# Four small edits to the order of work in a one-core encoder layer: VectorE for the first low parts, longer counted filter taps, a sixth early gate, pinned splits

## The chip, the cores and the metric

The kernel runs on one core of a Trainium2 chip. The metric is the device time of one execution in microseconds; smaller is better. The program has one launch and no arithmetic on the host.

## The reference: what is computed

One layer of a streaming Conformer with two mixers, on 2048 prompt rows and 64 sample rows (2112 in all), in float32, with D = 1024, eight heads of 64, 512 filter channels and an FFN of 2816. Cut to its core:

```python
sh1, sc1, gt1, sh2, sc2, gt2 = split(silu(c) @ w_ada + b_ada, 6)
h = rms_norm(x, norm1_g) * (1 + sc1) + sh1
glu_a, glu_b, q, k, v, g_conv, g_attn = split(h @ w_in)          # 512 512 512 512 512 1024 1024
u = glu_a * sigmoid(glu_b)
y = depthwise_conv(concat([hist, u]), w_dw) + b_dw               # 31 taps, causal, each channel alone
conv_out = silu(layer_norm(y, conv_ln_g, conv_ln_b)) @ w_conv_out
q, k = rms_norm(q per head), rms_norm(k per head)
s = q @ k.T / 8 + rel_bias[clip(distance, -128, 128)]            # own chunk of 64 and the 8 before it
attn_out = softmax(masked s) @ v @ w_attn_out
x = x + gt1 * ((sigmoid(g_conv) * conv_out + sigmoid(g_attn) * attn_out) @ w_o)
h2 = rms_norm(x, norm2_g) * (1 + sc2) + sh2
gate, up = split(h2 @ w_ffn_in)
y_out = x + gt2 * ((silu(gate) * up) @ w_ffn_out)
```

The sample rows have modulation, filter history and keys of their own. The last 30 filter inputs and the last keys and values are outputs as well.

## The kernel before

**Precision.** Each float32 product is made of three TensorE matmuls on operands that are split into a high part (ScalarE's copy to the short type `fp32r`) and a low part (operand minus high part, a subtraction). `mm3` issues hi x hi, hi x lo, lo x hi, in this order, so the low part of the left operand is needed by the third matmul.

**Phase 1** walks four row blocks (`PBLOCKS`, 576 or 512 rows) through the stages of `ORDER`: q, filter channels 0, k, 1, v, 2, 3, and then the two branch gates, g. The first block begins with the modulation columns `A` and `B` (small VectorE steps on `cols`), which make the transposed input `h` with its halves `hh` and `hl` and the first q product. `glu` makes 128 filter channels, `convolve` filters them with 31 VectorE instructions that all update one tile `y` (480 of them are the `scalar_tensor_tensor` form), and `conv_norm` makes the LayerNorm once the four channel groups are there and stores the result to `c_d`. Attention runs beside: `sc` are the scores, `pr` the exponentials, `sm` the row statistics, `ptp` the transposed probabilities, `o_p` the output of a head.

**Phase 2** walks three row blocks (`CBLOCKS`, 704, 640, 768 rows). Each makes the two branch projections and their merge in two chunks (`merge`), multiplies by `w_o`, and then runs one generator `residual` per 128 rows, a "turn": residual, norm, transposes into `pw`, and the split into FFN operands. The FFN's gate and up projections multiply 2 x 2 blocks (two halves of the rows, two halves of D) with seven products in place of eight, after Winograd, so the operands are `b11`, `b21`, `b22` and the sums `t1` to `t4` of the rows, and the weights `a11`, `a12`, `a22` and the sums `s1` to `s4`. GpSimd makes the sums of weights in `Weights.operand` (tile `ws`) in the first row block, and they are stored to `sum_d`, from where the other two blocks load them.

**The early gates.** The products with `a11` and `a12` need only `b11` and `b21`, which are ready before the `t` operands. For the first `EARLY` = 5 of the 22 slabs of 128 FFN columns they are done ahead: `first(f)` (with `a11`, key `fi`, 12 matmuls into a bank of tag `y`, of which there are four, then a copy to the tile `early`) and `second(f)` (with `a12`, 12 matmuls, then SiLU). Three firsts and two seconds come before the rest of the turns is drained, `first(3), first(4), second(2), second(3), second(4)` after it, with a call of `W.fill()` behind each. The main loop `up(f)` then starts at f = 0 with `s3` times `t3`; for f of 5 and more it does `a11` and `a12` itself.

**The order of the work.** Instructions are emitted by one Python program, which keeps a planned clock: every operation adds an estimate to `Stream.load` of its engine (`Meter`, `Stream.add`: a VectorE step on n elements counts 75 + 1.04 n ns), and no engine's clock stands behind TensorE's. Side work lives in generators on `Lane`s, which are pumped whenever TensorE's planned clock has moved by 500 ns; the lane of filter taps goes on while VectorE's planned clock is at most `CONV_ROOM` = 2000 ns ahead of TensorE's, up to four taps at a time. `conv.drain()` emits what is left at fixed places: at channel group 0 of the next block and, in the last block, at gate 10 (`SIDE_G`), just before the loads of the next phase (`load_mixed`, tile `cin`). `Stream.at` puts a step at a planned time. Behind the emission the tile framework orders the instructions of each engine by its own estimates, so the order of an engine is not that of the emission unless an edge demands it.

**The weights.** `Weights` loads slabs into three staging buffers (`wst`) by SyncE's queue, splits each into `whi` and `wlo` (five buffers each), stores the halves that later blocks need, and loads them from there. `split` chooses who makes the low part: VectorE for the slabs of `w_in` from the fifth on (`i >= 4`) and for every second slab of `w_o`, GpSimd for the rest. `fill` makes the next splits while a buffer is free and `available` agrees: while `hold` is set no `up` slab is split, and while turns are left (`careful`) a first `up` slab is split only if its loads and weight sums are there by the planned clock. `self.made` keeps the planned time of each sum, and `fill` is called then and when a slab has landed. `then`, at the planned end of a split, stores the halves and calls `presum`, which makes the next weight sums.

Of the kernel before, what the change touches and what calls it, by code (L numbers as in the profile page):

```python
# [8 lines left out]
F32 = mybir.dt.float32  # L9
# [7 lines left out]
P = 128  # L17
# [40 lines left out]
SCORE_ROOM = {"dve": 2500}  # L58
TURN_NS = 600.0
KEPT = ("qkv", "in", "fi", "fo")  # L60
EARLY = 5


def token_tiles(lo, hi):
# [185 lines left out]
class Weights:  # L250
# [2 lines left out]

    def __init__(self, engines, pool, dram, stream, keys, source, staging, held, kept):
        self.stream = stream
        self.sync, self.act, self.dve, self.gps = engines
        self.pool, self.dram, self.keys, self.source = pool, dram, keys, source
        self.staging, self.held = staging, held  # L260
        self.sum_pool, self.sum_d, self.sums, self.hold, self.landed = None, None, {}, 0, {}
        self.made, self.careful = {}, lambda: False
        self.room, self.leaving = {"wst": staging, "wup": 0, "wfo": 0}, {"wst": 0, "wup": 0, "wfo": 0}
        times, raws = {}, {}
        self.items, self.users, self.need, self.first, self.stored = [], [], {}, set(), {}
# [64 lines left out]
    def load(self, kind, sure=True):  # L330
        tag = self.free_tag(kind, sure)
        i = self.due[kind].pop(0)
        srcs, a, b = self.source(self.items[i])
        pool, bufs = (self.pool, self.staging) if tag == "wst" else (self.sum_pool, self.extra[tag])
        st = pool.tile([P, a, b], F32, tag=tag, name=tag, bufs=bufs)
        for j, src in enumerate(srcs):
            self.sync.dma_start(st[:, j * a // len(srcs) : (j + 1) * a // len(srcs)], src)
        self.loaded[i] = st, tag
        self.room[tag] -= 1
        self.landed[i] = self.stream.load["pe"] + DMA_LAG  # L340
        if self.items[i][0] == "fi":
            self.stream.at(self.landed[i], self.presum, True)
            self.stream.at(self.landed[i], self.fill, True)
        self.fill()

    def load_on(self, kind):
# [19 lines left out]
    def operand(self, f, op):  # L366
# [6 lines left out]
        while len(made) < int(op[1]):  # L373
            j = len(made)
            t = self.sum_pool.tile([P, 4, P], F32, tag="ws", name="ws", bufs=4)
            x, y, e = (
                lambda: (u[:, :4], u[:, 4:], ALU.add), lambda: (made[0], g[:, :4], ALU.subtract),
                lambda: (g[:, :4], u[:, :4], ALU.subtract), lambda: (g[:, 4:], made[1], ALU.subtract),
            )[j]()
            self.gps.tensor_tensor(t, x, y, e)  # L380
            made.append(t)
            self.made[f, j] = self.stream.when("pool")
            self.stream.at(self.made[f, j], self.fill, True)
            for c in self.parts_of(f, f"s{j + 1}"):
                self.drop(self.raws[c], "pool")
            self.stream.at(
                self.stream.when("pool"), lambda j=j, t=t: self.sync.dma_start(self.sum_d[f][j], t), True
            )
# [10 lines left out]
    def split(self):  # L399
# [10 lines left out]
        if not its:  # L410
            for t, d in zip((hi, lo), self.stored[key][0]):
                self.sync.dma_start(t.bitcast(F32), d)
            return
        e, name = (self.dve, "dve") if i >= 4 and key[0] in ("in", "qkv") or key[0] == "wo" and key[1] % 2 else (self.gps, "pool")
        if i in self.first:
            parts = [(slice(4 * j, 4 * j + 4), self.operand(f, op)) for j, (f, op) in enumerate(key[1:])]
            self.stream.after("act", "pool")
# [1 line left out]
            n = 4 if key[0] == "fi" else shape[1]  # L419
            parts = [(slice(j, j + n), self.loaded[its[0]][0][:, j : j + n]) for j in range(0, shape[1], n)]  # L420
        for c, src in parts:
            self.act.activation(hi[:, c], src, AF.Copy)
            self.stream.after(name, "act")
            e.tensor_tensor(lo[:, c], src, hi[:, c].bitcast(F32), ALU.subtract)
        if i in self.first:
# [17 lines left out]
    def available(self):  # L443
        i = len(self.ready)
        if i >= len(self.keys):
            return False
        if i in self.need:
            now = self.stream.load["pe"]
            if not self.there(i) or self.hold and self.keys[i][0] == "up":
                return False  # L450
            if i not in self.first or not self.careful():
                return True
            return all(self.landed[j] <= now for j in self.need[i]) and all(
                self.made.get((f, int(op[1]) - 1), 1e18) <= now for f, op in self.keys[i][1:] if op[0] == "s"
            )
        return self.keys[i] in self.stored

    def fill(self):
# [75 lines left out]
def streaming_layer(ctx: ExitStack, tc: tile.TileContext, I, O):  # L534
    nc = tc.nc
# [572 lines left out]
    def convolve(u, y, ct, b):  # L1108
# [13 lines left out]
        dve.tensor_scalar(y[:, ct, :n], u[:, :n], wd[:, ct, 0:1], bdw[:, ct : ct + 1], ALU.mult, ALU.add)  # L1122
        for k in range(1, TAPS):
            dve.scalar_tensor_tensor(y[:, ct, :n], u[:, k : k + n], wd[:, ct, k : k + 1], y[:, ct, :n], ALU.mult, ALU.add)
            yield

    def conv_norm(y, c0, n, t0):
# [304 lines left out]
    xs = first_rows()  # L1432
    M = Slabs(nc.sync, wa, stream, list(mod_order()), source, 4)
    M.fill()
    W = Weights((nc.sync, act, dve, gps), wpool, dram, stream, list(weight_order()), source, 3, 5, lambda key: key[0] in KEPT)
    first_block(xs)
    norm_lane.add(cached_kv())
    mods = mod_steps()
# [63 lines left out]
    work = Lane({}, 600.0)  # L1502
    turns = Lane({}, TURN_NS, wide=2)
    stream.lanes = [turns, work]

    W.careful = lambda: bool(turns.gens)

    def drain():
        turns.drain()
# [130 lines left out]
    for s, (lo, hi) in enumerate(CBLOCKS):  # L1640
# [52 lines left out]
                turns.add(gens[i])  # L1693

        hid = [wk.tile([P, 2, 2, CW], F32R, tag="m0", name="hid"), None]
        early = wk.tile([P, 2 * EARLY - 2, CW // 2], F32, tag="m1", name="early")
        early = [[early[:, 2 * f + j] for j in range(2)] for f in range(EARLY - 1)]
        early.append([piece("t2", "early") for _ in range(2)])
        acc = [None] * len(tiles)

        def product(ps, w, b, first, last):
# [167 lines left out]
        if not s:  # L1869
            W.open("fo", "wfo")  # L1870
        turns.drain()
        for step, f in ((first, 3), (first, 4), (second, 2), (second, 3), (second, 4)):
            step(f)
            W.fill()
        for f in range(0, NF, 2):
# [48 lines left out]
```

## Time and profile before

| | |
|---|---|
| Time, median of 3 runs | 3055.79 us (3053.33 to 3057.89) |
| The profiled execution's own time | 3054.2 us |
| Its span | 3052.4 us |
| Its mean granted TensorE clock | 0.988 |
| TensorE busy | 2961.2 us, 16403 matmuls |
| VectorE busy | 1781.9 us, 3431 instructions |
| ScalarE busy | 1179.4 us, 2110 instructions |
| GpSimd busy | 1044.0 us, 646 instructions |
| Filter taps (480 instructions of VectorE) | 368.4 us, mean 771 ns |
| Moved by DMA | 676.27 MB, mean 222 GB/s |

The span is the profiler's, from the first to the last instruction of the core; the time of the execution has 1.8 us around it. Busy times are sums over instructions of one execution. "PEld" in the rows is the loading of weights into TensorE, which runs beside its matmuls; DVE is VectorE, ACT is ScalarE, POOL is GpSimd, SP is SyncE, whose queue issues the DMAs. The granted clock is TensorE's as a share of full speed. L101 is the line of a helper through which every operation goes, so tiles, not lines, tell the operations apart.

### The profile page before, as it was taken

Reading aid. Unit: us, or ns where it says so; the run is one execution under the profiler, and the core shown is the slowest. Engines: PE = TensorE matmul, PEld = TensorE weight load, DVE = VectorE, ACT = ScalarE, POOL = GpSimd, SP = SyncE. Lnnn points to the kernel's source line nnn. Section 1 sums busy time; section 2 is a strip of 40 time slices with the busy share of each in tenths; the row PEclk is TensorE's granted clock in tenths of the full one; section 3 lists DMA queues with packets and bytes.
Section 4 is the critical chain, followed back from the end, with each engine's and each line's share of the span. In section 5 each row is a group of like instructions: output and inputs, shape, how many; then the busy total and the mean of one; then the engine's idle time right before and its main releaser. Section 6 shows DMA issues by size and latency. Waiting matters only on the chain.

```text
span 3052.4 us, 44465 instructions
## 1 busy us (share of the span) xinstructions
PE 2961.2 (97%) x16403; PEld 2634.7 (86%) x16403; DVE 1781.9 (58%) x3431; ACT 1179.4 (39%) x2110; POOL 1044.0 (34%) x646
## 2 busy tenths in 40 slices
PE   6989898999999999998999999999999999999999
PEld 4879776888888788898999998989999999999998
DVE  4798677877977895454443436554444556343345
ACT  2324532353245257455334343443333244322321
POOL 1300120111011102348778774344445343333431
PEclk9999999999999999999999999999999999999999
DMA  9788788887987689867455469754444965333434
GB/s 309 259 290 290 244 276 268 279 266 255 310 283 247 232 277 285 267 229 238 168 188 175 149 206 332 240 175 152 152 152 142 343 209 194 125 116 129 139 113 160
DMA packets 480167, 676.27 MB, mean 222 GB/s; under 512 B 37716, under 2 KB 316104, under 8 KB 479949
## 3 DMA queue, kind: packets, MB, share of 16 engines
q1 hardware_dynamic: 467669, 656.04, 65.3%
q10 hardware_dynamic: 12280, 17.39, 1.6%
q8 instruction: 129, 2.11, 0.3%
q14 instruction: 89, 0.73, 0.1%
HBM read 501.70 MB, written 171.61 MB: 221 GB/s over the span
## 4 chain that ended last, share of the span: by engine, by line
PE 82%; DVE 10%; DMA 3%; POOL 2%; issue 1%; ACT 1%; SPq 0%; ACTq 0%; DVEq 0%; POOLq 0%
PE ps L101 52%; PE pd L101 17%; PE pw L101 6%; DVE y L101 4%; PE po L101 2%; PE sc L101 2%; PE ptp L101 2%; PE pt L101 1%; DVE pr L101 1%; POOL r L101 1%; PE pa L101 1%; POOL wlo L101 1%; DVE wlo L101 1%; ACT whi L101 0%; DMA tg<-g_d 0%
## 5 line engine op out<-in xcount | busy, mean ns | idle before, releaser
L101 POOL TENSOR_TENSOR wlo<-wst,whi 128x1024 fp32r<-128x1024 f32 (+1 forms) x217 | 461.2, 2135 | 597.0 <-ACT whi L101 482.9
L101 PE MATMUL ps<-t,whi 128*128 128x352 f32 (+2 forms) x2112 | 510.1, 325 | 9.0 <-ACT t L101 4.9
L101 PE MATMUL pd<-whi,hid 128*128 128x512 f32 (+1 forms) x1496 | 466.2, 390 | 0.0
L101 ACT ACTIVATE whi<-wst 128x1024 fp32r<-128x1024 f32 (+1 forms) x270 | 260.5, 973 | 456.7 <-PE pd L101 180.3
L101 PE MATMUL ps<-b,whi 128*128 128x352 f32 (+2 forms) x1584 | 381.4, 324 | 2.3 <-ACT early L101 1.7
L101 PEld LDWEIGHTS ps<-t,whi 128*128 128x128 f32 x2112 | 371.2, 189 | 13.7 <-ACT t L101 5.7
L101 DVE SCALAR_TENSOR_TENSOR y<-u,wd,y 128x512 f32<-128x512 f32 (+1 forms) x480 | 368.4, 771 | 6.5
L101 PE MATMUL ps<-hh,whi 128*128 128x512 f32 (+2 forms) x992 | 364.7, 368 | 0.0
L101 PE MATMUL ps<-hl,whi 128*128 128x512 f32 (+2 forms) x992 | 347.6, 350 | 0.0
L101 PE MATMUL ps<-hh,wlo 128*128 128x512 f32 (+2 forms) x992 | 346.6, 349 | 0.4 <-DVE wlo L101 0.4
L101 PE MATMUL ps<-t,wlo 128*128 128x352 f32 (+2 forms) x1056 | 342.0, 324 | 0.1
L101 PEld LDWEIGHTS pd<-whi,hid 128*128 128x128 f32 (+1 forms) x1496 | 276.1, 185 | 62.7 <-issue 0.3
L101 DVE TENSOR_TENSOR acc<-acc,pd 128x512 f32<-128x512 f32 (+1 forms) x272 | 186.9, 687 | 207.6 <-PE pd L101 206.8
L101 PE MATMUL pd<-wlo,hid 128*128 128x512 f32 (+1 forms) x748 | 291.9, 390 | 0.7 <-DMA wlo<-w_dfo_l 0.7
L101 PEld LDWEIGHTS ps<-b,whi 128*128 128x128 f32 x1584 | 276.6, 188 | 3.9 <-ACT early L101 2.7
L101 PE MATMUL ps<-b,wlo 128*128 128x352 f32 (+2 forms) x792 | 256.3, 324 | 0.0
L101 POOL TENSOR_TENSOR r<-t,mhalf 128x8 f32<-128x8 f32 (+3 forms) x68 | 86.9, 1280 | 400.4 <-DVE t L101 384.1
L101 POOL TENSOR_TENSOR wlo<-wup,whi 128x1024 fp32r<-128x1024 f32 (+1 forms) x73 | 158.8, 2176 | 171.5 <-ACT whi L101 170.4
L101 PEld LDWEIGHTS ps<-hh,wlo 128*128 128x128 f32 x992 | 188.4, 190 | 23.2 <-DVE wlo L101 0.6
L101 PEld LDWEIGHTS ps<-hh,whi 128*128 128x128 f32 x992 | 189.3, 191 | 18.5 <-issue 2.1
L101 PEld LDWEIGHTS ps<-hl,whi 128*128 128x128 f32 x992 | 189.3, 191 | 15.5 <-issue 1.7
L101 PEld LDWEIGHTS ps<-t,wlo 128*128 128x128 f32 x1056 | 200.3, 190 | 0.4 <-POOL wlo L101 0.4
(206 smaller groups left out, 5431.1 us busy)
## 6 DMA issues: line engine op xcount, KB each, us to landing
whi<-w_din_h SPq DMA_DIRECT2D x72, 512.0 KB, 6.6
wlo<-w_din_l SPq DMA_DIRECT2D x72, 512.0 KB, 6.6
wst<-sum_d SPq DMA_DIRECT2D x133, 256.0 KB, 2.9
wmod<-in_w_ada SPq DMA_DIRECT2D x48, 512.0 KB, 7.8
sum_d<-ws SPq DMA_DIRECT2D x88, 256.0 KB, 4.6
whi<-w_dfo_h SPq DMA_DIRECT2D x44, 512.0 KB, 5.2
wlo<-w_dfo_l SPq DMA_DIRECT2D x44, 512.0 KB, 6.5
wst<-in_w_ffn_in SPq DMA_DIRECT2D x83, 256.0 KB, 3.3
```

The costliest lines, as they stand in the source:

```text
L101: return f(*args, **kw)
```

## The change

Four edits, and what they take with them:

- `EARLY` is 6. The sixth early gate needs room: the tile `m1` holds the results of four early gates, the pieces `t3` and `t2` those of the fifth and sixth. The list behind the drained turns becomes first(3), first(4), second(2), second(3), first(5), second(4), second(5).
- Each tap adds 170 ns (`TAP_NS`) to VectorE's planned clock.
- The low parts of the first four slabs, too, are made by VectorE.
- ScalarE's splits of the first `up` slabs that begin with f of 0 or 1 get `tc.keep_in_program_order`: an edge that keeps the instruction behind the one that the program emitted for the same engine just before it.
- `careful`, `made` and the calls of `fill` at landing times and planned ends of sums are taken out.

```diff
@@ constants
-EARLY = 5
+EARLY = 6
+TAP_NS = 170.0
@@ Weights
-    def __init__(self, engines, pool, dram, stream, keys, source, staging, held, kept):
-        self.stream = stream
+    def __init__(self, engines, pool, dram, stream, keys, source, staging, held, kept, pin):
+        self.stream, self.pin = stream, pin
...
-        self.made, self.careful = {}, lambda: False
@@ Weights.load
             self.stream.at(self.landed[i], self.presum, True)
-            self.stream.at(self.landed[i], self.fill, True)
@@ Weights.operand
-            self.made[f, j] = self.stream.when("pool")
-            self.stream.at(self.made[f, j], self.fill, True)
@@ Weights.split
-        e, name = (self.dve, "dve") if i >= 4 and key[0] in ("in", "qkv") or key[0] == "wo" and key[1] % 2 else (self.gps, "pool")
+        e, name = (self.dve, "dve") if key[0] in ("in", "qkv") or key[0] == "wo" and key[1] % 2 else (self.gps, "pool")
...
-            self.act.activation(hi[:, c], src, AF.Copy)
+            ins = self.act.activation(hi[:, c], src, AF.Copy)
+            if i in self.first and key[1][0] < 2:
+                self.pin(ins)
@@ Weights.available
-            now = self.stream.load["pe"]
             if not self.there(i) or self.hold and self.keys[i][0] == "up":
                 return False
-            if i not in self.first or not self.careful():
-                return True
-            return all(self.landed[j] <= now for j in self.need[i]) and all(
-                self.made.get((f, int(op[1]) - 1), 1e18) <= now for f, op in self.keys[i][1:] if op[0] == "s"
-            )
+            return True
@@ convolve
             dve.scalar_tensor_tensor(y[:, ct, :n], u[:, k : k + n], wd[:, ct, k : k + 1], y[:, ct, :n], ALU.mult, ALU.add)
+            stream.load["dve"] += TAP_NS
             yield
@@ streaming_layer
-    W = Weights((nc.sync, act, dve, gps), wpool, dram, stream, list(weight_order()), source, 3, 5, lambda key: key[0] in KEPT)
+    W = Weights(
+        (nc.sync, act, dve, gps), wpool, dram, stream, list(weight_order()), source, 3, 5, lambda key: key[0] in KEPT,
+        tc.keep_in_program_order,
+    )
...
-    W.careful = lambda: bool(turns.gens)
...
-        early = wk.tile([P, 2 * EARLY - 2, CW // 2], F32, tag="m1", name="early")
-        early = [[early[:, 2 * f + j] for j in range(2)] for f in range(EARLY - 1)]
-        early.append([piece("t2", "early") for _ in range(2)])
+        early = wk.tile([P, 2 * EARLY - 4, CW // 2], F32, tag="m1", name="early")
+        early = [[early[:, 2 * f + j] for j in range(2)] for f in range(EARLY - 2)]
+        early += [[piece(tag, "early") for _ in range(2)] for tag in ("t3", "t2")]
...
-        for step, f in ((first, 3), (first, 4), (second, 2), (second, 3), (second, 4)):
+        for step, f in ((first, 3), (first, 4), (second, 2), (second, 3), (first, 5), (second, 4), (second, 5)):
             step(f)
             W.fill()
```

## The prediction

> **What bounds the kernel now.** First the page's busy shares.
>
> ```profile
> PE 2961.2 (97%) x16403; PEld 2634.7 (86%) x16403; DVE 1781.9 (58%) x3431; ACT 1179.4 (39%) x2110; POOL 1044.0 (34%) x646
> ```
>
> TensorE is busy for 2961.2 of 3052.4 us, so all its idle time together is 91.2 us, and no edit here takes a matmul away. What can be won is idle time of TensorE, and the slow clock that follows it. The view of windows tells where both lie (us, then busy time of PE, PEld, DVE, ACT and POOL, granted clock, share of DMA, GB/s):
>
> ```profile
> 0.00:50.00 50.00, 30.73 (x167) 16.83 (x171) 20.43 (x54) 15.91 (x31) 13.86 (x18) 1.00 0.90 301
> 200.00:250.00 50.00, 43.54 (x286) 40.44 (x287) 46.09 (x104) 17.67 (x42) 1.90 (x3) 0.90 0.75 255
> 450.00:550.00 100.00, 89.14 (x481) 70.63 (x481) 76.06 (x164) 22.40 (x52) 4.35 (x8) 0.91 0.84 285
> 1360.00:1425.00 65.00, 57.07 (x319) 53.58 (x318) 42.10 (x80) 39.77 (x81) 55.59 (x45) 0.95 0.77 264
> 1985.00:2010.00 25.00, 21.85 (x138) 20.65 (x137) 20.65 (x37) 14.94 (x31) 13.40 (x6) 0.93 0.57 183
> 2540.00:2600.00 60.00, 59.70 (x330) 56.67 (x329) 40.08 (x71) 33.97 (x60) 22.99 (x11) 1.00 0.55 193
> ```
>
> Four places answer to the four edits: the start, where TensorE idles 19.3 of 50 us; the filter stretches of the first phase (200 to 250, 450 to 550), idle for 17.3 us of 150 at a clock of 0.90 and 0.91; the entry to the first FFN block (1360 to 1425), idle for 7.9 us at 0.95; and the entry to the second (3.2 us at 0.93). The entry to the third has 0.3 us to give. The rows below are from the timelines of these stretches, the groups and the chain of waits.
>
> **The start: low parts of the first four slabs on VectorE.** In a timeline row stand start, duration, engine, line, operation, tiles, and in brackets the idle time before it and who ended it.
>
> ```profile
> 21.14 4.65 POOL L101 TENSOR_TENSOR wlo<-wst,whi 128x1024 fp32r<-128x1024 f32 x2 [5.76 <-ACT whi L101]
> 28.84 2.35 POOL L101 TENSOR_TENSOR wlo<-wst,whi 128x1024 fp32r<-128x1024 f32 x1 [3.05 <-ACT whi L101]
> 23.49 2.32 DVE L101 TENSOR_TENSOR A<-A,cols 128x4 f32<-128x4 f32 x1
> 43.18 0.16 DVE L101 TENSOR_TENSOR A<-A,cols 128x4 f32<-128x4 f32 x1
> 28.91 2.89 DVE L101 TENSOR_TENSOR hl<-h,hh 128x576 fp32r<-128x576 f32 x1
> 33.47 0.76 DVE L101 TENSOR_TENSOR hl<-h,hh 128x576 fp32r<-128x576 f32 x1 [0.75 <-ACT hh L101]
> 31.86 0.69 PE L101 MATMUL ps<-whi,hl 128*64 128x512 f32 x1 [1.11 <-DVE hl L101]
> 46.33 1.23 DVE L101 TENSOR_TENSOR wlo<-wst,whi 128x1024 fp32r<-128x1024 f32 x1 [0.19 <-ACT whi L101]
> ```
>
> A VectorE step on 128x4 elements takes 0.16 us at 43.18 and 2.32 us at 23.49, where it ends (25.81) within 0.02 us of the end of the two GpSimd subtractions (25.79). hl takes 0.76 at 33.47 and 2.89 at 28.91, beside the GpSimd step that begins at 28.84. VectorE stands while GpSimd works, and both steps are on the path: A makes the first h, and TensorE waits 1.11 us for hl. Without GpSimd's work the A step wins 2.16 us and TensorE's wait for hl goes, 1.11: 3.3 us. Against it, four steps of 1.23 us enter VectorE's queue; two of them become ready about when B and A do, and can push these back by some 0.4 us each. I take -2.5. The ends: all four on the path, 4.9 - 3.3 = +1.6; both VectorE delays won whole, 2.16 + 2.13 = -4.3. The four remaining slabs' DMAs and their stores stay where they are on SP's queue; the stores wait for a low part that is ready 1.1 us sooner. Everything behind follows the start, so the gain is kept.
>
> The Trainium skill has the same as a rule (SBUF — State Buffer, "Who interferes with whom"): a VectorE instruction with two SBUF inputs and a GpSimd instruction that reads SBUF exclude each other, and the later of them "fully blocks". The trace agrees, 2.32 against 0.16 us; by the rule alone this part would bring its far end, -4.3.
>
> **The filter: 170 ns more for each tap in the planner's VectorE clock.** No instruction changes; what changes is where the code puts taps between other steps, since their lane stops when VectorE's counted load is 2 us ahead of TensorE's.
>
> ```profile
> L101 DVE SCALAR_TENSOR_TENSOR y<-u,wd,y 128x512 f32<-128x512 f32 (+1 forms) x480 | 368.4, 771 | 6.5
> PE ptp L101 <- DVE pr L101: 9.9, 6, 5.9
> PE sc L101 <- DVE sm L101: 9.2, 9, 2.6
> 487.44 0.75 DVE L101 SCALAR_TENSOR_TENSOR y<-u,wd,y 128x512 f32<-128x512 f32 x1
> ...
> 488.92 0.37 DVE L101 TENSOR_SCALAR pr<-pr,sm 64x320 f32<-64x320 f32 x1
> 489.44 0.55 PE L101 MATMUL ptp<-ident,pr 64*128 64x64 f32 x3 [5.85 <-DVE pr L101]
> ```
>
> The planner counts 75 + 1.04 x 512 = 607 ns for a tap that takes 771; with 170 more it counts 777. A run of 30 taps is thus planned 30 x 0.164 = 4.9 us too short, about the longest wait (5.85 us, of softmax's small steps behind taps). From 100 to 1250 us TensorE waits 9.9 + 9.2 = 19.1 us for softmax on VectorE. The slow clock beside it, 0.10 x 50 + 0.09 x 100 = 14 us of lost clock, belongs to those waits in good part. So there are at most some 30 us to win. But VectorE's order is not the emission's: a tap needs only the tap before it, and the tool that orders each engine fills VectorE with taps wherever it thinks it free. Counting a tap 28% longer (777 / 607) thins the taps ahead of a softmax step by a fifth, not more: 0.22 x 30 = 6.6. I take -6, rounded down. The ends are -20 (two thirds) and +14 (below). What is hidden: the filter itself ends later, by the argument of the second rival.
>
> **Entry to the first FFN block: EARLY = 6, the pins, no `careful`.** `careful` held back a split of sums while turns were left. Without it nothing is emitted sooner here: until the turns are drained the sixth gate's slab takes the fifth buffer, so I cost its removal at nothing; without that cover it would move one s3 split ahead, which the pin places anyhow.
>
> ```profile
> 1380.71 1.15 ACT L101 ACTIVATE whi<-ws 128x512 fp32r<-128x512 f32 x2 [1.46 <-POOL ws L101]
> 1382.64 0.42 ACT L101 ACTIVATE pw<-pw,B,A 128x128 f32<-128x128 f32 x1
> 1387.81 0.59 PE L101 MATMUL ps<-b,whi 128*128 128x352 f32 x2 [1.58 <-ACT early L101]
> 1392.46 0.43 PE L101 MATMUL ps<-t,whi 128*128 128x352 f32 x1 [0.50 <-ACT t L101]
> 1394.81 0.66 PE L101 MATMUL ps<-t,whi 128*128 128x352 f32 x1 [1.92 <-DVE t L101]
> 1400.66 0.69 DVE L101 TENSOR_TENSOR pw<-pw,b 128x512 f32<-128x512 f32 x1
> 1405.09 0.63 ACT L101 ACTIVATE whi<-ws 128x512 fp32r<-128x512 f32 x1 [3.11 <-POOL ws L101]
> 1406.84 0.58 ACT L101 ACTIVATE t<-pw 128x512 fp32r<-128x512 f32 x1
> 1407.47 0.43 PE L101 MATMUL ps<-t,whi 128*128 128x352 f32 x1 [2.99 <-ACT t L101]
> 1408.20 17.11 PE ps L101 x95
> 1441.67 19.33 PE ps L101 x120
> L101 POOL TENSOR_TENSOR wlo<-ws,whi 128x512 fp32r<-128x512 f32 x13 | 17.0, 1325 | 0.7 <-ACT whi L101 0.7
> ```
>
> A product is 12 matmuls: 19.33 / 10 = 1.93 us. The last t operand could start when VectorE is done at 1401.35; ScalarE starts it at 1406.84, since splits of weight sums, which wait for GpSimd, stand ahead of it (1405.09, 3.11 us). That costs the 2.99 us at 1407.47. The 1.92 at 1394.81 is VectorE's own chain. The window idles 65.00 - 57.07 = 7.9 us in all and loses 0.05 x 65 = 3.2 of clock: 11 us is the ceiling.
>
> The sixth gate puts two products, 3.86 us, ahead of the first use of t; they leave the main loop (its steps a11 and a12 for f = 5), so TensorE's total stays. In block 0 GpSimd makes two more low parts first (2 x 1.325 us) and the main loop two fewer; one load and two stores of the sixth gate join SP's queue ahead of the loads that the sums need, with 0.23 of the DMA time free here. All this ends before the pinned wait below, which hides it; without that cover it would cost the 2.6 us.
>
> The pins hold the splits of f = 0 and 1 behind what ScalarE got just before them in the code. The first, s3 of f = 0, is emitted after the last t split, so it leaves its place at 1380.71 and goes behind t. This frees ScalarE: pw at 1382.64 no longer waits behind these splits and comes some 2.4 us earlier, and with it the chain to t: 1401.35 - 2.4 = 1399.0, t until 1399.5, s3's high part until 1400.1, its low part (1.325 on GpSimd) until 1401.4. TensorE has done its early products at 1392.46 - 0.50 = 1391.96 now; without the 1.58 and with 3.86 more that is 1394.2, and it waits some 7 us. The third matmul of a product takes the low part, so the first product ends near 1401.4 + 1.6 = 1403.0, and the eleven others before the first down projection at 1403.0 + 11 x 1.93 = 1424.2; at the clock lost now for each idle microsecond (3.2 / 7.9) the 7 cost 2.8 more: 1427.0. In the kernel before these twelve end at 1408.20 + 17.11 = 1425.3, with the two products still to come, so at 1429.2. That is -2. The ends are -11 (t and s3 are there when the products end) and +1 (t as late as now, until 1401.9, and the 1.58 kept: the low part at 1403.9, 8.1 us of waiting, the end at 1430.0).
>
> The Trainium skill (TensorE: Matmul & The Clock Gate, "Why this matters for your kernels") wants no TensorE gap over about 3 us, as one idle window halves the clock. Waits of 1.92 and 2.99 us came with 0.95 here, so shorter ones do it too; the rule speaks against gathering them into one wait of 7 us.
>
> **Entry to the second block.**
>
> ```profile
> 1996.43 0.41 PE L101 MATMUL ps<-t,whi 128*128 128x320 f32 x1 [1.40 <-ACT t L101]
> 2001.20 0.47 DVE L101 SCALAR_TENSOR_TENSOR early<-tg,ps 128x320 f32<-128x320 f32 x1
> ```
>
> Here sums come from DRAM and nothing is pinned. At 320 columns a product is 1.93 x 320 / 352 = 1.75 us, two are 3.5 us, against 3.2 us of idling. But four `y` banks serve six gates, so the first product with t now needs the bank of the fourth gate, whose SiLU ends at 2001.67. By then TensorE has done 12 products in place of 11. I take one product, 1.75 us, and a little clock: -2 (ends: -5, all idle time and clock, and 0). The third block has no wait to hide: 0.
>
> **Sum.** -2.5 - 6 - 2 - 2 = -12.5. The profiled execution took 3054.2 us, 1.6 less than the median of 3055.8; against the median that is 3043.
>
> **The rivals.** 0.2%, some 6 us, is about what a measurement of this kernel can tell from no change.
>
> *The planner's clock does nothing* (0.22): VectorE fills itself with taps as before, and the pinned wait eats the two products. Left are the start and the second block, -2.5 - 2 = -4.5: 3051. For it speaks that a tap already stands between softmax's small steps wherever VectorE pauses (487.44, ahead of 488.92).
>
> *The last filter runs over its drain* (0.13), slower:
>
> ```profile
> 1143.01 1.54 DVE L101 SCALAR_TENSOR_TENSOR y<-u,wd,y 128x512 f32<-128x512 f32 x2
> 1149.04 0.92 SPq L1001 DMA_DIRECT2D cin<-c_d  x2
> 1234.86 0.56 PE L101 MATMUL ps<-cin,whi 128*128 128x320 f32 x2 [1.40 <-DVE o_p L101]
> 1237.88 0.38 SPq L1181 DMA_DIRECT2D c_d<-part_l  x1
> ```
>
> The taps of the last block end at 1144.5, just before the drain whose first load is at 1149.04; its LayerNorm stores until 1237.9, while the next phase starts at 1234.86. Taps thinned by a fifth over 60 x 0.75 = 45 us end 10 to 14 us later, the rest is put in one lump before softmax, and the LayerNorm comes out behind the phase's end. It decides once the last tap passes 1149 and the wait at 1235 grows with it: +14, less 2.5 and 2 elsewhere, 3065. Against it: after 1150 VectorE is less loaded, and TensorE has gate products to do.
>
> *The waits at the FFN all close* (0.10): -11 and -5 in place of -4, 3031.
>
> **Numbers.** The forecast has 0.55 (3034 to 3049), the rivals 0.22, 0.13 and 0.10. Range 3027 to 3061. Faster 0.70 (forecast, the third rival, some of the first); same 0.18; slower 0.12.
>
> **What would show it.** Right: A<-A,cols near 25 us at about 0.16 us; TensorE idle from 0 to 100 us less by 2 to 3; waits for pr and sm from 100 to 1250 under 16 us in all; at the first FFN entry one wait of 5 to 8 us for a whi or wlo in place of three, t splits ahead of the first ws split; at the second a wait for an early bank. Wrong: waits for softmax of 20 us or more, taps after 1149 with a wait over 5 us near 1235, or splits of sums still ahead of t.

## The result and the profile after

The changed kernel takes 3073.75 us (median of 8 runs, 3064.34 to 3081.24) where the kernel before takes 3056.17 (8 runs beside it, 3046.78 to 3059.44): 1.0057 times as long, with a 95% interval of 1.0039 to 1.0075. It is slower, outside the predicted range, and the prediction had the other sign.

The profiled execution took 3073.06 us with a span of 3071.3, 18.9 more than before. First two rows of its page, the busy shares and the group with the longest waits; then the view of windows (us, busy time of PE, PEld, DVE, ACT and POOL, granted clock, share of DMA, GB/s) at the places that the prediction looked at, moved along with the later stages:

```profile
PE 2963.4 (96%) x16403; PEld 2638.0 (86%) x16403; DVE 1789.8 (58%) x3441; ACT 1176.6 (38%) x2102; POOL 1020.7 (33%) x640
L102 PE MATMUL ps<-t,whi 128*128 128x352 f32 (+2 forms) x2112 | 510.9, 326 | 17.5 <-ACT hid L102 9.9
```
```profile
0.00:50.00 50.00, 31.69 (x184) 17.24 (x184) 23.77 (x64) 16.18 (x32) 4.49 (x14) 1.00 0.93 308
200.00:250.00 50.00, 44.58 (x278) 42.17 (x279) 44.47 (x99) 19.87 (x46) 1.41 (x3) 0.83 0.71 242
450.00:550.00 100.00, 89.42 (x489) 69.03 (x487) 87.98 (x182) 22.86 (x54) 4.44 (x8) 0.93 0.85 280
1232.00:1270.00 38.00, 32.06 (x191) 29.40 (x190) 21.95 (x38) 14.53 (x23) 9.77 (x5) 0.91 0.77 255
1370.00:1445.00 75.00, 59.56 (x333) 56.82 (x332) 41.68 (x80) 40.46 (x83) 57.31 (x45) 0.86 0.66 228
2000.00:2030.00 30.00, 27.05 (x169) 26.54 (x168) 20.89 (x38) 19.37 (x37) 14.58 (x6) 0.89 0.60 217
```

TensorE has the same work (2963.4 against 2961.2 us busy), so the loss is idle time and what it does to the clock. The start is better (GpSimd is busy for 4.49 us in place of 13.86, TensorE idles 18.3 in place of 19.3). The filter stretches, taken together, are as they were (idle for 16.0 us in place of 17.3, at a lower clock in the first and a higher one in the second), and TensorE's waits for softmax between 100 and 1250 us (total, times, longest) sum to 21.6 us in place of 19.1:

```profile
PE sc L102 <- DVE sm L102: 17.3, 10, 7.9
PE ptp L102 <- DVE pr L102: 4.3, 3, 3.0
```

Two places are worse: the entry to the first FFN block, idle for 15.4 us of 75 at a clock of 0.86, and the entry to the merge (1232 to 1270), which in the kernel before is:

```profile
1232.00:1270.00 38.00, 34.81 (x220) 32.11 (x219) 21.73 (x38) 13.13 (x20) 14.30 (x7) 1.00 0.87 302
```

Stage lengths of the profiled executions tell the same. They are read from the first matmul on `cin` of each row block (start of its merge) and the first on `b` and `whi` (start of its FFN); "end" is the last matmul. Each row is one execution, and even where no edit acts such lengths differ by up to 3 us (block 1: 544.4 before, 547.5 with the pins alone):

| us | to first `cin` | to first `b` | FFN of block 0 | block 1 | block 2 to end |
|---|---|---|---|---|---|
| before | 1234.9 | 132.8 | 493.0 | 544.4 | 642.3 |
| changed kernel | 1238.7 | 137.5 | 501.2 | 545.8 | 643.6 |
| low parts alone | 1232.1 | 132.1 | 492.7 | 545.6 | 642.4 |
| filter count alone | 1244.6 | 137.1 | 494.0 | 545.5 | 642.4 |
| sixth gate alone | 1236.5 | 132.4 | 485.7 | 542.9 | 641.9 |
| pins alone | 1235.7 | 133.5 | 503.8 | 547.5 | 642.4 |

The changed kernel loses 3.9 + 4.6 us up to the first FFN block and 8.2 in it. Where the last went can be read from the timelines of GpSimd, ScalarE, VectorE and TensorE at the entry to the first FFN block (start, duration, engine, line, operation, tiles, and in brackets the idle time before it and who ended it):

```profile
1393.88 1.29 POOL L102 TENSOR_TENSOR ws<-wup,ws 128x512 f32<-128x512 f32 x1
1407.14 2.51 POOL L102 TENSOR_TENSOR wlo<-ws,whi 128x512 fp32r<-128x512 f32 x2 [11.97 <-ACT whi L102]
...
1405.95 0.60 ACT L102 ACTIVATE t<-pw 128x512 fp32r<-128x512 f32 x1 [1.09 <-DVE pw L102]
1406.44 1.66 ACT L102 ACTIVATE whi<-ws 128x512 fp32r<-128x512 f32 x3
1419.66 0.63 ACT L102 ACTIVATE whi<-ws 128x512 fp32r<-128x512 f32 x1 [0.84 <-POOL ws L102]
1427.07 0.63 ACT L102 ACTIVATE whi<-ws 128x512 fp32r<-128x512 f32 x1 [6.77 <-POOL ws L102]
1429.78 0.44 ACT L102 ACTIVATE hid<-ps 128x352 fp32r<-128x352 f32 x1
...
1418.34 0.53 DVE L102 TENSOR_TENSOR ps<-ps,early 128x352 f32<-128x352 f32 x1
...
1407.11 0.96 PE L102 MATMUL ps<-t,whi 128*128 128x352 f32 x2 [4.60 <-ACT whi L102]
1433.41 0.93 PE L102 MATMUL ps<-t,whi 128*128 128x352 f32 x2 [9.92 <-ACT hid L102]
```

The pin does what it says: the first split of a sum (1406.44) stands behind the last `t` (1405.95). TensorE waits 4.60 us once, as was expected. But GpSimd had made four sums by 1395.2, as many as there are `ws` tiles. Its next instruction is the low part of the first of them, which needs ScalarE's split, so it stood for 11.97 us. It then works without a pause, and is late: ScalarE reaches the first split of a sum of f = 2 and waits 6.77 us for that sum. Behind that split, in ScalarE's queue, stands `hid`, whose input VectorE had ready at 1418.87. It starts at 1429.78, and TensorE, which needs its bank, waits 9.92 us.

### The profile page after: what moved, and what is told of

It reads as the page before. It is cut to its first block, busy times and chain, and to the rows that moved or that the text cites. A ratio compares the mean times of both kernels' runs of the same rounds, so it can differ in the third digit from the quotient of the medians.

```text
span 3071.3 us, 44477 instructions
## 1 busy us (share of the span) xinstructions
PE 2963.4 (96%) x16403; PEld 2638.0 (86%) x16403; DVE 1789.8 (58%) x3441; ACT 1176.6 (38%) x2102; POOL 1020.7 (33%) x640
## 4 chain that ended last, share of the span: by engine, by line
PE 53%; DMA 2%; DVE 1%; ACT 1%; POOL 1%; issue 0%; SPq 0%; ACTq 0%; POOLq 0%; DVEq 0%
PE ps L102 32%; PE pd L102 16%; PE pw L102 5%; DMA wst<-in_w_attn_out 1%; DMA wst<-in_w_o 0%; DVE pw L102 0%; ACT whi L102 0%; DMA tg<-g_d 0%; POOL wlo L102 0%; DVE t L102 0%; ACT xn L102 0%; PE pt L102 0%; POOL ws L102 0%; DMA wlo<-w_dfo_l 0%; DVE b L102 0%
## 5 line engine op out<-in xcount | busy, mean ns | idle before, releaser
L102 POOL TENSOR_TENSOR wlo<-wst,whi 128x1024 fp32r<-128x1024 f32 (+1 forms) x210 | 442.8, 2119 | 550.7 <-ACT whi L102 485.5
L102 POOL TENSOR_TENSOR r<-t,mhalf 128x1 f32<-128x1 f32 (+3 forms) x68 | 81.8, 1205 | 355.1 <-DVE t L102 331.1
```

What stands on the lines that cost most here:

```text
L102: return f(*args, **kw)
```

## The experiments

**Each edit alone, on the kernel before.** The low parts:

```diff
-        e, name = (self.dve, "dve") if i >= 4 and key[0] in ("in", "qkv") or ...
+        e, name = (self.dve, "dve") if key[0] in ("in", "qkv") or ...
```

> The kernel before with the low parts of its first four slabs on VectorE and nothing else. Theory (each edit has its own effect; the loss is made by the filter clock and the pins): the first store of normalised keys (pt<-kn, 88.06 us before, 80.44 after) comes near 80 us as in the changed kernel, and most of it lasts: 4 to 8 us faster than before, near 3049. Rival (the start's gain is taken back by any later order of phase 1): the early gain is there at 80 us and gone by 1235 us; within 2 us of before.

3051.27 us (11 runs) against 3055.45 of before: 0.9990, interval 0.9982 to 0.9999. That is 3 to 4 us, at or under the lower end of the theory. In four profiles with this edit (low parts alone 80.62, changed kernel 80.44, without the pins 77.79, low parts and sixth gate 81.20) the first transposes of `kn` start at 80.0 us in the mean; in four without it (before 88.06, filter count 83.90, sixth gate 85.27, pins 87.22) at 86.1; the other profiles agree (77.6 to 80.1 with it, 84.2 to 86.7 without). So some 6 us are won by then, and the first matmul on `cin` has 2.8 of them left (1232.1 for 1234.9): the rival has its part. The row of the changed kernel that the prediction named has come out:

```profile
23.19 0.16 DVE L102 TENSOR_TENSOR A<-A,cols 128x4 f32<-128x4 f32 x1
```

The filter count:

```diff
+            stream.load["dve"] += TAP_NS        # 170.0, behind each tap
```

> The kernel before with 170 ns more for each tap in the planned VectorE clock and nothing else. Theory (the longer count moves the emission of the last LayerNorm, not the taps): the last tap still ends near 1143 us, y<-y,pm comes near 1190 us in place of 1164, the merge waits about 4 us more for c_d, the first FFN product starts 8 to 12 us later than before: 8 to 14 us slower. Rival (the prediction's: softmax waits are closed): waits for pr and sm between 100 and 1250 us fall from 19 to under 16 us, 3 to 8 us faster. Rival 2 (nothing but reshuffled waits): within 3 us.

3070.28 us: 1.0044 (1.0030 to 1.0058), 13 us slower. Timelines of VectorE (the last taps, the first LayerNorm step, the merge's first step `t`) and TensorE (the merge), and the waits for softmax and LayerNorm between 100 and 1250 us (total, times, longest):

```profile
1143.05 0.75 DVE L102 SCALAR_TENSOR_TENSOR y<-u,wd,y 128x512 f32<-128x512 f32 x1
1195.39 1.88 DVE L102 TENSOR_TENSOR y<-y,pm 128x512 f32<-128x512 f32 x3 [4.83 <-PE pm L102]
1244.61 0.56 PE L102 MATMUL ps<-cin,whi 128*128 128x320 f32 x2 [1.40 <-DVE o_p L102]
1255.40 0.49 DVE L102 SCALAR_TENSOR_TENSOR t<-tg,ps 128x320 f32<-128x320 f32 x1 [2.36 <-DMA c_d<-part_l]
1255.94 0.90 PE L102 MATMUL ps<-cin,whi 128*128 128x320 f32 x2 [4.03 <-DVE t L102]
...
PE sc L102 <- DVE sm L102: 14.7, 8, 7.9
PE pm L102 <- POOL s L102: 7.0, 1, 7.0
PE ptp L102 <- DVE pr L102: 3.8, 3, 3.0
```

In the kernel before the same rows are:

```profile
1163.69 2.48 DVE L101 TENSOR_TENSOR y<-y,pm 128x512 f32<-128x512 f32 x4 [0.75 <-PE pm L101]
1240.82 0.49 DVE L101 SCALAR_TENSOR_TENSOR t<-tg,ps 128x320 f32<-128x320 f32 x1 [1.64 <-DMA c_d<-part_l]
1246.51 0.56 PE L101 MATMUL ps<-cin,whi 128*128 128x320 f32 x2 [0.82 <-DVE t L101]
```

The last tap ends at 1143.8, as before (1144.5). The LayerNorm's first step behind it comes 31.7 us later than before. So does, by some 15 us, what hangs on its last store (`c_d<-part_l`): `t`, VectorE's first step of the merge, waits for that store to land and starts at 1255.40 in place of 1240.82, and TensorE waits 4.03 us for it. The softmax waits are 18.5 us in place of 19.1, so nothing is won there, and a wait of 7.0 us for another LayerNorm's sum is new.

The sixth gate (its tiles and list, held-back splits kept):

```diff
-EARLY = 5
+EARLY = 6
-        for step, f in ((first, 3), (first, 4), (second, 2), (second, 3), (second, 4)):
+        for step, f in ((first, 3), (first, 4), (second, 2), (second, 3), (first, 5), (second, 4), (second, 5)):
```

> The kernel before with EARLY = 6 (its tiles and its list) and nothing else; the held-back splits and their calls of fill stay. Theory (the pins, not the sixth gate, idle GpSimd): no wait over 4 us between 1365 and 1440 us, the waits for t in the first FFN block smaller than before: 2 to 6 us faster, up to 3 lost at the second block's entry, so 0 to 5 faster. Rival (two more low parts on GpSimd ahead of the sums make them late): a wait for hid or whi of 6 to 10 us near 1425, 4 to 8 us slower.

3045.99 us: 0.9970 (0.9959 to 0.9981), 9 us faster, more than either theory gave. The window of the entry, first of the kernel before and then of this one, the two longest of TensorE's remaining waits there, and the one at the second block's entry:

```profile
1360.00:1435.00 75.00, 67.07 (x363) 61.26 (x362) 42.97 (x81) 44.60 (x90) 63.14 (x50) 0.95 0.77 266
```
```profile
1360.00:1435.00 75.00, 70.85 (x403) 64.86 (x402) 43.31 (x83) 47.54 (x97) 64.07 (x50) 1.00 0.79 270
```
```profile
1396.79 0.59 PE L101 MATMUL ps<-t,whi 128*128 128x352 f32 x2 [0.78 <-DVE early L101]
1413.17 0.59 PE L101 MATMUL ps<-t,whi 128*128 128x352 f32 x2 [1.80 <-DVE u L101]
...
1995.17 0.56 PE L101 MATMUL ps<-t,whi 128*128 128x320 f32 x2 [2.95 <-DVE early L101]
```

Without the pins the two products do cover the `t` operands, and the clock stays whole.

The pins:

```diff
-            self.act.activation(hi[:, c], src, AF.Copy)
+            ins = self.act.activation(hi[:, c], src, AF.Copy)
+            if i in self.first and key[1][0] < 2:
+                self.pin(ins)
```

> The kernel before with the splits of the first sums of f = 0 and 1 kept behind the ScalarE instruction emitted before them, and nothing else (five early gates). Theory (the pins hold the first ws splits behind the last t, so GpSimd, whose four ws tiles are full, stands idle for about 10 us and the sums run late behind it): GpSimd idle 8 to 13 us in one piece before 1410, a wait for t or s3 of 6 to 9 us at about 1393 to 1405 and a second wait of 5 to 10 us for hid near 1420: 8 to 14 us slower. Rival (the order alone helps as predicted; the loss is the sixth gate's): the waits of 1.58, 1.92 and 2.99 us become one of 4 to 7 us and nothing follows: within 3 us.

3068.48 us: 1.0041 (1.0025 to 1.0056), 12 to 13 us slower. GpSimd's timeline, TensorE's, and the window:

```profile
1382.19 1.29 POOL L101 TENSOR_TENSOR ws<-wst,ws 128x512 f32<-128x512 f32 x1
1399.86 2.51 POOL L101 TENSOR_TENSOR wlo<-ws,whi 128x512 fp32r<-128x512 f32 x2 [16.38 <-ACT whi L101]
...
1399.84 0.95 PE L101 MATMUL ps<-t,whi 128*128 128x352 f32 x2 [8.23 <-ACT whi L101]
1426.13 0.93 PE L101 MATMUL ps<-t,whi 128*128 128x352 f32 x2 [9.45 <-ACT hid L101]
```
```profile
1360.00:1435.00 75.00, 56.41 (x312) 53.21 (x311) 39.87 (x77) 40.15 (x82) 52.15 (x42) 0.86 0.60 204
```

Both waits are there without the sixth gate, with GpSimd idle for 16.38 us; the two more products shorten it to 11.97 and the first wait to 4.60. The four ratios multiplied give 1.0045; the change measures 1.0057 (1.0039 to 1.0075).

**Is GpSimd's lateness the cause of the second wait?** The pins, and the low parts of the pinned slabs on VectorE:

```diff
-... or key[0] == "wo" and key[1] % 2 else (self.gps, "pool")
+... or key[0] == "wo" and key[1] % 2 or i in self.first and key[1][0] < 2 else (self.gps, "pool")
```

> The kernel before with the pins, as in the run with the pins alone, and the low parts of the pinned slabs (f = 0 and 1, ten parts) made by VectorE in place of GpSimd. Theory (the second wait comes from GpSimd being late by the 16 us that the first pin kept it idle): GpSimd has 10 x 1.3 = 13 us less to do, the wait for hid near 1426 falls from 9.45 us to under 4; the first wait (8.23 us) stays over 5, since it is for the high part; 6 to 10 us faster than with the pins alone, 3058 to 3062. Rival (ScalarE's order is the fault: hid stands behind splits of f = 2 whatever GpSimd does): the wait for hid stays over 7 us and the time near 3068.

3061.22 us: 1.0015 (1.0006 to 1.0024). The first wait is as it was, the second is gone:

```profile
1398.56 0.96 PE L101 MATMUL ps<-t,whi 128*128 128x352 f32 x2 [8.23 <-ACT whi L101]
1409.58 0.59 PE L101 MATMUL ps<-t,whi 128*128 128x352 f32 x2 [2.70 <-DVE u L101]
```

GpSimd stands here too, for 17.26 us. But with 13 us of work taken off it, `hid` starts 1.8 us after its input is ready in place of 10.4, so the second wait comes from GpSimd's lateness, worth some 7 us, and the first from the pin itself.

**The changed kernel without the pins** (the two lines with `self.pin(ins)` taken out):

> The changed kernel without the pins (four edits left: low parts, filter clock, sixth gate, no held-back splits). Theory (the pins' loss of 12 to 13 us is the same beside the other edits): the wait of 9.9 us for hid near 1433 is gone and GpSimd's idle 12 us too, 10 to 14 us faster than the changed kernel: 3058 to 3063. Rival (without the held-back splits the first splits come too early and block ScalarE before t in the pins' place): a wait of 4 us or more for t between 1395 and 1430, within 6 us of the changed kernel.

3059.87 us: 1.0005 (0.9996 to 1.0014), 14 us faster than with them, as the theory had it. **Without the longer count as well:**

> The changed kernel without the pins and without the longer count: low parts, sixth gate, and no held-back splits. Theory (taking the held-back splits out does nothing while the sixth gate's slab fills the fifth buffer): same as the low parts and the sixth gate alone, 3041 to 3048. Rival (it sets free a split of sums that blocks ScalarE): 4 us or more slower than that, with a wait of over 2 us for t near 1400.

3043.81 us: 0.9952 (0.9940 to 0.9964). That is the kernel with the low parts, the sixth gate and no held-back splits. **With held-back splits kept, the two edits that gained:**

> The kernel before with the two edits that gained alone, the low parts and the sixth gate. Theory (their places, 0 to 80 us and 1380 to 1425 us, lie apart, so the gains add): 3.5 to 4.5 + 9 = 11 to 14 us faster than before, 3041 to 3045, the fastest of all so far. Rival (the earlier start is lost again before the FFN, as part of it was alone): 7 to 10 us faster, no better than the sixth gate alone.

3044.83 us: 0.9955 (0.9941 to 0.9968). The gains add as expected, and taking out `careful` does nothing that these runs tell apart.

**Where the longer count costs.** The last row block alone:

```diff
+            stream.load["dve"] += TAP_NS * (b + 1 == len(PBLOCKS))
```

> The kernel before with the 170 ns counted for the taps of the last row block alone. Theory (the last block's LayerNorm is emitted later because the planned clock says that VectorE is not done): y<-y,pm comes 20 us or more later than in the kernel before (1164) though the last tap ends near 1143 as there, the wait for the tile t at the merge is 4 us, the first FFN product starts 8 to 12 us later, nothing changes before 1090 us: 8 to 12 us slower than before, most of the 13 to 15 that the count costs in all four blocks. Rival (the loss lies in the waits of 7.0 us for pm near 391 and 7.9 us for sm near 524): neither wait is there and the time is within 3 us of before.

3067.03 us: 1.0029 (1.0020 to 1.0039), 10 us slower. The size was right, the account only in part: the LayerNorm step is late by 9 us, not 20 (1172.64), the wait for `t` is 1.47 us, not 4, and what is late first is attention: its first `cin` comes at 1244.42, and a wait for softmax has no gate product beside it. The waits of 7.0 and 7.9 us that the rival named are not there, so it is out:

```profile
1214.44 1.44 PE L102 MATMUL sc<-kk,q 128*128 128x320 f32 x4 [3.37 <-DVE sm L102]
1244.42 0.56 PE L102 MATMUL ps<-cin,whi 128*128 128x320 f32 x2 [1.40 <-DVE o_p L102]
1252.65 0.49 DVE L102 SCALAR_TENSOR_TENSOR t<-tg,ps 128x320 f32<-128x320 f32 x1 [2.42 <-DMA c_d<-part_l]
```

So I gave the last block's attention a wider room:

```diff
                     attention(b)
+                    ATTN["dve"], SCORE_ROOM["dve"] = (4000, 3500) if b == 3 else (3000, 2500)
```

> As the run that counts 170 ns more for the taps of the last row block alone, and attention of that block may run when the planned VectorE clock is up to 4000 ns (scores: 3500) ahead of TensorE's, in place of 3000 (2500). Theory (the longer count fills the planned room that taps and attention share, so attention falls behind the gates, and its last steps have no gate product beside them): with the room widened attention keeps its place, the first matmul on cin comes within 4 us of the kernel before (1235 us, 1244 with the count alone), 5 to 9 us faster than with the count alone, 3058 to 3062. Rival (the late LayerNorm alone decides): first matmul on cin still near 1244 or a wait of over 3 us for t near 1250, 3065 to 3069.

3066.78 us: 1.0035 (1.0022 to 1.0047), no faster than with the count alone. Attention did come back (first `cin` at 1239.03), and then the merge waited for its step `t`, which waits for the LayerNorm's last store:

```profile
1253.48 0.49 DVE L102 SCALAR_TENSOR_TENSOR t<-tg,ps 128x320 f32<-128x320 f32 x1 [3.59 <-DMA c_d<-part_l]
1254.02 0.90 PE L102 MATMUL ps<-cin,whi 128*128 128x320 f32 x2 [7.67 <-DVE t L102]
```

The rival's sign, a wait of over 3 us for `t`, and its time came out. My theory had the place of attention right and the time wrong: attention and LayerNorm are both late, and although attention ends 5 us earlier with the wider room, `t` starts no earlier (1253.48 for 1252.65). The room by itself:

> The kernel before with the wider room for the last block's attention and taps counted as before. It tells what the room does by itself. Theory (attention of the last block isn't held back in the kernel before): within 3 us of before. Rival (room is worth something by itself): 4 us or more faster, and then the run with both tells nothing of the count.

3056.30 us: 1.0006 (0.9995 to 1.0017), nothing.

**A series of counts**, each with the low parts and the sixth gate:

```diff
+TAP_NS = -100.0        # then -200.0, 85.0, and -100.0 in the last row block alone
```

> The kernel before with the low parts, the sixth gate, and taps counted 100 ns shorter than before (507 for a measured 771), the opposite of the edit. Theory (the count is a share of a common budget, not a time that must be true): attention and the LayerNorm of the last block are emitted no later than before, the entry to the merge is no later, and the time is within 4 us of the two edits alone, 3041 to 3049. Rival (a truer count is better, the prediction's reason): the waits for pr and sm grow by 6 us or more and it is 5 to 10 us slower than the two edits alone, 3050 to 3055.

> The low parts and the sixth gate, and taps counted 200 ns shorter (407 for a measured 771). Theory (the count sets how early the taps, and with them the LayerNorm behind them, are emitted, and a shorter one is better until taps crowd softmax out): y<-y,pm of the last block at 1125 to 1140 us or earlier, waits for pr and sm not above 30 us, 3026 to 3036. Rival (any other count only reshuffles; the 3032.7 at 100 ns less was luck): anywhere from 3036 to 3060, out of order with the other counts.

> The low parts and the sixth gate, and taps counted 85 ns longer, half of the edit. Theory (the loss grows with the count): y<-y,pm of the last block between 1160 and 1190 us, time between the 3044.8 of no extra count and the 3059.9 of 170: 3047 to 3058. Rival (only a reshuffle): outside of these, most likely equal to or below 3045.

> The low parts and the sixth gate, and taps counted 100 ns shorter in the last row block alone. Theory (the last block's LayerNorm and attention make most of the difference, as with the longer count): first matmul on cin 5 to 10 us earlier than with the two edits alone (1233 us), 3034 to 3040. Rival (the gain of 12 us lies in the softmax waits of the earlier blocks, 485 us above all): within 3 us of the two edits alone, 3042 to 3048.

| ns added | last tap ends | first `y<-y,pm` | first `cin` | time, us | ratio to before (interval) |
|---|---|---|---|---|---|
| -200 | 1144.7 | 1147.2 | 1247.2 | 3058.00 | 1.0009 (0.9996 to 1.0021) |
| -100 | 1127.2 | 1139.6 | 1218.1 | 3032.65 | 0.9919 (0.9906 to 0.9933) |
| -100, last block | 1135.5 | 1147.9 | 1226.8 | 3037.88 | 0.9940 (0.9928 to 0.9952) |
| 0 | 1140.5 | 1159.9 | 1233.3 | 3044.83 | 0.9955 (0.9941 to 0.9968) |
| 85 | 1146.6 | 1177.1 | 1248.2 | 3063.59 | 1.0025 (1.0015 to 1.0035) |
| 170 (no held-back splits) | 1143.8 | 1191.4 | 1239.3 | 3059.87 | 1.0005 (0.9996 to 1.0014) |

From -100 up the LayerNorm's first step comes later with each step of the count, as the mechanism wants; the time follows it from -100 to 85 and not to 170. At 85 the time lies above the theory's range; the rival had that it would leave the range, but looked for it at or below 3045. TensorE waits 16.1 us there for loads of keys (3.3 with the two edits alone), which neither had. At -200 the waits for softmax are 27.2 us (21.7 with the two edits alone), the LayerNorm's first step is no earlier than at -100, the time is where the rival had it, and my range is missed by 22 us. That the taps crowd softmax out there is not shown:

```profile
PE sc L102 <- DVE sm L102: 18.0, 9, 10.5
PE sc L102 <- DMA kk<-k_d: 16.1, 10, 3.9
```
```profile
PE sc L102 <- DVE sm L102: 20.6, 16, 4.4
PE ptp L102 <- DVE pr L102: 6.6, 5, 3.6
```

The first pair is the run at 85, the second that at -200. At -100 it is 12 us faster than with the two edits alone, where theory and rival gave none or a loss; 7 of these (5 by the ratios, whose intervals overlap) come with the shorter count in the last block alone, near what the last theory said. So the count moves the LayerNorm, but the time doesn't follow the count: a loss at -200 and a larger loss at 85 than at 170 are what the rival of a mere reshuffle would give, and it is not excluded. This version, at 0.9919 of the time before, is the fastest here and beats both kernels.

## Why the prediction was wrong

**The filter count** is the first step that failed. It was put at -6 us with ends of -20 and +14, and measures +13 alone. The step that failed is the reason: I took the softmax waits as what the count would change, and 0.22 x 30 us as the gain. Those waits stayed (18.5 for 19.1 us with the count alone, and 21.6 in the changed kernel, over the 20 that the prediction named as a sign of being wrong). The count moved what is emitted behind the taps and beside them: VectorE's planned clock is a room that attention shares, and the LayerNorm begins only when no tap is left to emit. The second rival named this place, at +14 and with a chance of 0.13, and its sum was right, in part by luck, since its mechanism was not: the taps don't end later and none passes 1149. What comes later is the LayerNorm behind them, by 31.7 us at its first step. The last row block alone makes 10 of the 13 us; that its late store holds back the merge is read from the rows of `t`, and no run gave the LayerNorm its old place under the longer count.

**The pins** are the second. The entry to the first FFN block was put at -2 (-11 to +1); in the changed kernel its FFN takes 8.2 us more. The steps up to the first wait held: one wait in place of three, `t` ahead of the first split of a sum, 4.60 us where about 7 were given, and 8.23 with the pins alone. What was left out is the other end of the same wait. The text said what ScalarE gains by the pin and not what GpSimd loses: it has four tiles for sums, fills them, and stands 12 us. I took GpSimd's later work as covered up to the first product, and it was uncovered 25 us further on. The Trainium skill (Perfetto Trace Analysis, "Per-engine timelines") has ScalarE and VectorE as strict first-in first-out queues; the trace agrees for ScalarE: `hid`, ready at 1418.87, starts at 1429.78 behind a split that waits for GpSimd.

**The sixth gate** was mis-sized downward because of that. I let the pinned wait eat its two products; without pins they are worth 9 us, near the -11 that I had as the far end, since the slow clock goes with the waits: 3.8 us less idling and, by the working in the last section, 3.3 us less lost clock. The note that gathering waits is dear did not come out as a matter of clock: 18.6 us of idling with the pins alone, nearly all in two waits, cost 4.4 us of clock, against 3.3 for 7.9 us before. What the pins cost is the idling itself. The Trainium skill's rule of gaps over 3 us (TensorE: Matmul & The Clock Gate, "Why this matters for your kernels") holds here for the waits of 8.23 and 9.45 us, but those of 1.92 and 2.99 us in the kernel before, both under it, were followed by a halved clock too.

**The second block's entry** went as written in its waits: one for an early bank (2.95 us) in place of two of 1.4 us. The -2 is not shown: block 1 is 1.5 us shorter with the sixth gate alone and 1.4 longer in the changed kernel, less than it varies where no edit acts.

**The start** was right in its mechanism (0.16 us for 2.32) and sign. -2.5 is near the 3 to 4 us of the time, in part by luck: by 80 us the gain is 6, more than the far end of -4.3, and about half of it is lost again before the merge. VectorE's order changed in the start too, and the waits for it at 55.34 and 73.72 us (1.95 and 1.62 us in the kernel before) shrank to 0.54 and 0.25 with the low parts alone, which no step of the sum had.

**No `careful`** at nothing: 3043.81 without it, 3044.83 with it.

What stays open: why 85 ns costs more than 170, and how much of any count's effect is the order that it happens to give. Why the low parts' gain shrinks from 6 to 3 us before the merge, and why block 1 is 3 us longer with the pins alone, where nothing is pinned, was not followed up.

## What to carry to other kernels

When an instruction is held back, price its producer as well as its consumer: an engine with a few output tiles stops when nobody empties them, and it shows as lateness well after the wait that was looked at. An estimate in a planner's clock is a share of a room and a date for what follows, not only a duration: the count that is truer to the trace (777 for 771 ns) was dearer than the false one (507), though a falser one still (407) lost all that the two other edits had gained, so ask first who shares the clock and who waits for its date. Take edits that travel together apart before believing in their sum: here two gained 12 us and two lost 26.

## What the runs showed of the hardware

Idle time of TensorE is followed by stretches at half clock, and what these cost depends on whether TensorE works in them. Windows of the kernel before, behind its waits of 1.92 and 2.99 us, and of the kernel with the pins alone, within its waits of 8.23 and 9.45 us (behind the window and its length stands TensorE's busy time; the granted clock is the third number from the end):

```profile
1394.80:1398.00 3.20, 3.19 (x11) 3.19 (x12) 3.20 (x4) 2.11 (x4) 3.20 (x3) 0.50 0.46 175
1408.50:1411.50 3.00, 3.00 (x11) 3.00 (x11) 0.07 (x1) 0.00 (x1) 2.73 (x3) 0.50 0.14 43
```
```profile
1396.00:1399.80 3.80, 0.00 (x0) 0.00 (x0) 3.14 (x6) 1.13 (x3) 0.00 (x0) 0.50 0.00 0
1419.50:1426.10 6.60, 0.00 (x0) 0.00 (x1) 2.46 (x6) 4.43 (x7) 6.60 (x6) 0.50 0.26 99
```

In the kernel before nearly all of the 6.8 us at half clock hit matmuls, and half of that time, 3.3 us, is lost. With the pins alone 20.5 us are slow, but TensorE stands in 11.7 of them, so only half of the other 8.8 is lost, 4.4 us. The mean clock of a window with long waits (0.86) therefore makes the loss look larger than it is: 0.14 x 75 would be 10.5 us. Idling and lost clock together are 11.3 us at this entry before, 23.0 with the pins alone and 4.2 with the sixth gate alone, where 4.2 us of idling, no wait over 1.80 us, came with a clock of 1.00. The differences, +11.7 and -7.1 us, fit the lengths of the FFN of block 0 (+10.8 and -7.3).
